# Steps of the mLSTM heads set behind the recurrence's bursts on TensorE

## The chip, the cores and the metric

One NeuronCore of a Trainium2 chip runs the whole program in one launch. The time is the device time of an execution in microseconds (us). TensorE (PE) multiplies, VectorE (DVE) and ScalarE (ACT) evict its results and do the elementwise work, GpSimd (POOL) does a little of it, SyncE (SP) issues the weight loads. [...]

## The reference

The input is 512 tokens of width 1024, in fp32. A first block has a hybrid token mixer, a cross attention to 256 memory rows and a gated FFN; a second block has three attention branches. The change touches the mixer alone. Half of the mixer's width is four mLSTM heads of 128 columns:

```
c_loc = einsum('bhclv,bhclk->bhcvk', v * wa[..., None], k)        # per chunk
c_new = s_old * c + s_loc * c_l                                   # state between chunks
p = exp(d - m_t) * einsum('bhctd,bhcsd->bhcts', q, k)
num = s_int * einsum('bhcvk,bhctk->bhctv', c_prev, q) + einsum('bhcts,bhcsv->bhctv', p, v)
h = num / max(|den|, exp(-m_t))                                   # then standardized per head
```

q, k, v and an output gate of each head are columns of `h @ w_in`. The other half is an RWKV-7 recurrence over eight heads of 64 (`state = state*w - (state kk)(kk a)^T + v k^T`), which is serial in time.

## The kernel before

The dense products split each fp32 operand in a high and a low part (`whi`, `wlo` of the weights, `hh`, `hl` of the activations) and take three products per 128 rows of weight: one *dense step* is three matmuls of 128x512 (`dense_steps`, `mmd`, L180). A block of 128 output columns is eight dense steps. ACT and DVE make `whi` and `wlo` from each loaded weight (L155, L158).

The mLSTM heads are two generators. `project(hd)` makes q, k, v and the gate of a head: four blocks, 32 dense steps; behind the k and q blocks `conv` does a width-4 convolution, on DVE three STTs (scalar_tensor_tensor instructions) of 128x512 (`k<-mc`, `q<-mc`) and one more (`k<-th`, `q<-th`). `attend(hd)` does the chunkwise attention of the head in ten steps, of which eight issue on TensorE: transposes of `cl` (the decay terms), transposes of `k2`, the product q k, four chunk steps c0 to c3, and, two empty steps later, the transposes of the normalized `Dm`. A chunk step c makes `vw` (weighted values, DVE, one buffer), the products `pn` (Vx by Dm), `pq` (C by q, from c1 on) and `pc` (vw by Kt, up to c2), then evicts: `nt` and the next state `C`, which `pq` of the next chunk step reads. Between c3 and the transposes of `Dm` some twenty small DVE instructions normalize the head.

`beside(gen, other, n)` joins the two: `project(hd + 1)` is the main stream, and `attend(hd)` is advanced by one step behind every third dense step (n = 32 // 10 = 3). Head 3's `attend` stands in the same way beside `mem_kv`, which makes keys and values for the cross attention and first needs the buffers `hh`.

`weave` interleaves that stream with the RWKV recurrence by progress. First comes `rwkv_inv`: a triangular solve in 31 rounds on DVE (`itmp`, `Tmat`, L158), with eight sets of four transposes of `Tmat` on TensorE. Then comes `rwkv_chain`: bursts of small matmuls that depend on each other through evictions: `columns` (transposes of BK and xT), `sides` (transposes of KR, products Z by Gm, copies to `rgu`), `solve` (rgu by TT, copies to `Z`), `step` (Z by St, q = 0 evicted by ACT, q = 1 by DVE: a copy to `Z` and one to `sg` or `yt`, L839), `ops` (St by Z, added to `St`). Between bursts `yield` lets the dense steps fill TensorE. In both stages `pinned` holds TensorE to the order in which the program is written; the queues of DVE and ACT are ordered by the scheduler, by priority in the order of writing and by readiness.

Of the kernel before, what the change touches and what calls it, by code (L numbers as in the profile page):

```python
# [41 lines left out]
MX = 2  # L42
# [21 lines left out]
            raise RuntimeError("every stream waits")  # L64


def beside(gen, other, n):

    for q, at in enumerate(gen):
        if q % n == n - 1:  # L70
            next(other, None)
        yield at
    for _ in other:
        pass


def weave(*gens):
    for _ in woven(*gens):
        pass


def part(gen, n):

    for _ in range(n):
        at = next(gen, "end")
        if at == "end":
            return
        yield at
# [11 lines left out]
class Build:  # L100
    def __init__(self, ctx, tc, ins, out):
        self.ctx, self.tc, self.nc = ctx, tc, tc.nc
        self.i, self.out = ins, out
        self.n = 0
        self.pinned = ""
        self.turns = ["p"]
        self.mms = ["mm"]
        self.const = ctx.enter_context(tc.tile_pool(name="const", bufs=1, reuse_waits=RW))

        self.wp = ctx.enter_context(tc.tile_pool(name="wp", bufs=2, reuse_waits=RW))  # L110
        self.wr = ctx.enter_context(tc.tile_pool(name="wr", bufs=2, side="right", reuse_waits=RW))
        self.banks = {}
        self.hb = ctx.enter_context(tc.tile_pool(name="hb", bufs=1))
        self.late = None
        self.before = None
# [26 lines left out]
    def units(self, n, gen, pri=0):  # L142

        q = 0
        while True:
# [4 lines left out]
            q += at is not None  # L150
            yield None if at is None else float(q) / n


    def act(self, out, in_, func=AF.Copy, **kw):
        self.pin("a", self.nc.scalar.activation(out, in_, func, **kw))  # L155
# [22 lines left out]
    def mmd(self, out, a, b, start, stop):  # L178

        ins = self.nc.tensor.matmul(out, lhsT=a, rhs=b, start=start, stop=stop)  # L180
        if "p" in self.pinned:
            self.pin("p", ins)
        elif self.before is not None:
            self.after(ins, self.before)
        self.before = ins.ins.name

    def mm(self, out, a, b, start=True, stop=True):
        self.pin("p", self.nc.tensor.matmul(out, lhsT=a, rhs=b, start=start, stop=stop))  # L188

    def tr(self, out, in_, ident=None):  # L190
        self.pin("p", self.nc.tensor.transpose(out, in_, self.ident if ident is None else ident))  # L191

    def after(self, ins, name):

        self.tc.add_manual_dep(ins.ins, name, mybir.DependencyInfo(
            mybir.DependencyClass.NoSync, mybir.DependencyReason.DATA), reason="dense order")
# [351 lines left out]
    def block(self, h, c0):  # L548
        wu = self.unit(self.i["w_in"][0][:, c0:c0 + 128], KD, 128)
        ps = self.pm()  # L550
        self.dense(ps, wu, h, range(KD))
        return ps
# [494 lines left out]
    def mlstm(self, ml, h, yT, hpool, kept):  # L1047
# [7 lines left out]
        def conv(ps, jb, tag):  # L1055
            cur = mt("mc", (128, 515), 1)
            nc.gpsimd.memset(cur[:, 0:3], 0.0)
            self.act(cur[:, 3:515], ps)
            acc = mt(tag, (128, 512), 2)
            self.act(acc, ps, AF.Identity, scale=v["m_conv_w"][:, 24 + jb:25 + jb], bias=v["m_conv_b"][:, jb:jb + 1])  # L1060
            for d in range(2, -1, -1):
                self.stt(acc, cur[:, d:d + 512], v["m_conv_w"][:, 8 * d + jb:8 * d + jb + 1], acc)
            th = mt("th", (128, 512), 1)
            self.act(th, acc, AF.Tanh, scale=0.5)
            self.stt(acc, th, 1.0, acc, OP.add, OP.mult)
            return acc
# [3 lines left out]
        def project(hd):  # L1070

            ps = yield from block(512 + 128 * hd)
            k2 = conv(ps, 4 + hd, "k2")
            ps = yield from block(128 * hd)
            q2 = conv(ps, hd, "q2")
            ps = yield from block(1024 + 128 * hd)
            vT = mt("vT", (128, 512), 1)
            self.act(vT, ps)
            og = yT[:, hd]
            gen = block(1536 + 128 * hd)  # L1080
            yield from part(gen, 3)
            p = self.pt("q")
            for c in range(NB):
                self.tr(p[:, 128 * c:128 * c + 128], vT[:, 128 * c:128 * c + 128])
            Vx = mt("Vx", (128, 4, 129), 2)
            nc.gpsimd.memset(Vx[:, :, 128:129], 1.0)
            self.act(Vx[:, :, 0:128], p.rearrange("p (c k) -> p c k", c=4))
            ps = yield from gen
            self.act(og, ps, AF.Tanh, scale=0.5)
            self.ts(og, og, 1.0, gh[:, hd:hd + 1], OP.add, OP.mult)  # L1090
            ops[hd] = (k2, q2, Vx)
# [80 lines left out]

        yield from project(0)
        for hd in range(3):
            yield from beside(project(hd + 1), attend(hd), 32 // (8 + MX))
        yield from beside(self.mem_kv(hpool, ml, kept), attend(3), 3)

    def sumsq(self, pool, x, g=None):

# [1037 lines left out]
```

## Time and profile before

| | us |
|---|---|
| time, median of 3 (lowest to highest) | 1542.51 (1539.69 to 1544.95) |
| the profiled execution, its own time | 1537.13 |
| its span, first to last instruction | 1535.4 |
| TensorE busy | 1506.9 |
| VectorE busy | 1082.0 |
| ScalarE busy | 748.7 |
| GpSimd busy | 98.9 |

The stage that the change touches lies at about 185 to 355 us of the span. A line of a timeline is the start, the duration, the engine, the source line, the operation, what it writes and reads, and its size; a bracket behind it is the idle time before it and what ended it. TensorE's matmuls overlap: the time that one takes of the engine is the distance to the next start, not its duration.

### The profile page before, as it was taken

To read this page: it belongs to the slowest core of one execution; us is meant where nothing else is said; L and a number is where in the kernel's file an instruction comes from. 1 tells how busy PE (TensorE), PEld (TensorE's weight loads), DVE (VectorE), ACT (ScalarE), POOL (GpSimd) and SP (SyncE) were. 2 spreads that over 40 slices of the span, in tenths; PEclk is the share of its full clock that TensorE was granted. 3 is DMA by queue.
4 is the path that set the end of the run, shared out by engine and by line. 5 is a ranking of instruction groups with operands and counts; after the bars stand their busy time and mean duration, and the time that the engine had idled before them with its cause. 6 is when DMAs were issued, how large, how long until landed. Compare 5 with 4: busy or idle time off the path is not lost.

```text
span 1535.4 us, 23728 instructions
## 1 busy us (share of the span) xinstructions
PE 1506.9 (98%) x8487; PEld 1237.2 (81%) x8487; DVE 1082.0 (70%) x2536; ACT 748.7 (49%) x1469; POOL 98.9 (6%) x241
## 2 busy tenths in 40 slices
PE   7999999999999999999999999999999999999999
PEld 5777788798888888888888888898877877878877
DVE  7776698998856556524544578879999785766563
ACT  6645556566554444434432444456554454644431
POOL 7000402122000000000000001000000000000000
PEclk9999999999999999999999999999999999999999
DMA  7533222145533133333333334242322322324222
GB/s 254 145 73 81 52 63 56 45 122 158 153 111 100 51 96 97 96 96 97 97 100 98 93 107 103 62 122 71 91 71 68 83 69 67 80 75 124 69 83 96
DMA packets 209591, 144.85 MB, mean 94 GB/s; under 512 B 13492, under 2 KB 190787, under 8 KB 208960
## 3 DMA queue, kind: packets, MB, share of 16 engines
q1 hardware_dynamic: 208000, 141.66, 32.6%
q0 software_dynamic: 1280, 1.52, 0.5%
q8 instruction: 67, 1.10, 0.3%
q14 instruction: 52, 0.43, 0.1%
q10 hardware_dynamic: 192, 0.14, 0.0%
HBM read 134.90 MB, written 8.39 MB: 93 GB/s over the span
## 4 chain that ended last, share of the span: by engine, by line
PE 85%; DVE 9%; ACT 2%; issue 1%; DMA 1%; DVEq 0%; SPq 0%; ACTq 0%
PE mm L180 39%; PE q L180 28%; PE p L188 4%; PE p L191 3%; PE y L188 3%; PE s L180 2%; DVE wlo L158 2%; PE s L188 2%; PE q L188 2%; PE s L191 1%; PE q L191 1%; DVE lqk L158 1%; DVE madd L1832 1%; ACT whi L155 1%; DVE m L1831 1%
## 5 line engine op out<-in xcount | busy, mean ns | idle before, releaser
L155 ACT ACTIVATE whi<-wraw 128x512 fp32r<-128x512 f32 (+2 forms) x472 | 292.5, 622 | 534.5 <-PE mm L180 216.2
L158 DVE TENSOR_TENSOR wlo<-wraw,whi 128x512 fp32r<-128x512 f32 (+2 forms) x472 | 320.3, 680 | 186.1 <-ACT whi L155 181.4
L180 PE MATMUL mm<-hh,whi 128*128 128x512 f32 (+1 forms) x760 | 281.2, 386 | 1.8 <-DVE hh L158 1.1
L180 PE MATMUL mm<-hh,wlo 128*128 128x512 f32 (+1 forms) x696 | 265.3, 381 | 0.0
L180 PE MATMUL mm<-hl,whi 128*128 128x512 f32 x632 | 247.2, 391 | 0.0
L180 PEld LDWEIGHTS mm<-hh,whi 128*128 128x128 f32 x760 | 138.9, 189 | 29.2 <-issue 3.0
L180 PEld LDWEIGHTS mm<-hh,wlo 128*128 128x128 f32 x696 | 131.0, 188 | 25.4
L180 PEld LDWEIGHTS mm<-hl,whi 128*128 128x128 f32 x632 | 119.2, 189 | 22.4 <-issue 0.5
L180 PE MATMUL q<-hh,whi 128*128 128x512 f32 x272 | 106.2, 391 | 0.0
L180 PE MATMUL q<-hh,wlo 128*128 128x512 f32 x272 | 106.0, 390 | 0.0
L180 PE MATMUL q<-hl,whi 128*128 128x512 f32 x272 | 106.0, 390 | 0.0
L180 PE MATMUL q<-whi,hh 128*128 128x512 f32 (+2 forms) x176 | 66.8, 388 | 0.0
L180 PE MATMUL mm<-whi,hh 128*128 128x512 f32 (+2 forms) x168 | 65.5, 396 | 0.0
L180 PE MATMUL q<-wlo,hh 128*128 128x512 f32 (+2 forms) x160 | 60.9, 381 | 0.0
L180 PEld LDWEIGHTS q<-hh,wlo 128*128 128x128 f32 x272 | 51.1, 188 | 10.6
L180 PEld LDWEIGHTS q<-hl,whi 128*128 128x128 f32 x272 | 51.1, 188 | 10.5
L180 PEld LDWEIGHTS q<-hh,whi 128*128 128x128 f32 x272 | 51.1, 188 | 10.4
L180 PE MATMUL mm<-wlo,hh 128*128 128x512 f32 (+2 forms) x152 | 57.9, 381 | 0.0
L180 PE MATMUL q<-whi,hl 128*128 128x512 f32 (+2 forms) x144 | 54.7, 380 | 0.0
L180 PE MATMUL mm<-whi,hl 128*128 128x512 f32 (+2 forms) x136 | 51.6, 380 | 0.0
L155 ACT ACTIVATE at_sm<-at_sm,at_mx 128x128 f32<-128x128 f32 (+3 forms) x64 | 35.7, 559 | 21.3 <-DVE at_mx L1598 20.9
L176 DVE SCALAR_TENSOR_TENSOR fy<-fc,vcols,fy 128x512 f32<-128x512 f32 x44 | 33.0, 751 | 9.2 <-ACT fy L155 8.5
(761 smaller groups left out, 3123.3 us busy)
## 6 DMA issues: line engine op xcount, KB each, us to landing
wraw<-in_w_in_dram SPq DMA_DIRECT2D x172, 256.0 KB, 2.9
wraw<-in_f_up_dram SPq DMA_DIRECT2D x88, 256.0 KB, 2.9
wraw<-in_f_down_dram SPq DMA_DIRECT2D x40, 256.0 KB, 2.8
wraw<-in_x_wkv_dram SPq DMA_DIRECT2D x32, 256.0 KB, 3.1
wraw<-in_w_out_dram SPq DMA_DIRECT2D x32, 256.0 KB, 2.7
wraw<-in_w_branch_dram SPq DMA_DIRECT2D x24, 256.0 KB, 2.7
wraw<-in_w_mem_kv_dram SPq DMA_DIRECT2D x16, 256.0 KB, 4.3
wraw<-in_x_wq_dram SPq DMA_DIRECT2D x16, 256.0 KB, 2.8
```

The source lines that it names most:

```text
L155: self.pin("a", self.nc.scalar.activation(out, in_, func, **kw))
L158: self.pin("v", self.nc.vector.tensor_tensor(out, a, b, op=op))
L176: self.pin("v", self.nc.vector.scalar_tensor_tensor(out, a, s, b, op0=op0, op1=op1))
L180: ins = self.nc.tensor.matmul(out, lhsT=a, rhs=b, start=start, stop=stop)
L188: self.pin("p", self.nc.tensor.matmul(out, lhsT=a, rhs=b, start=start, stop=stop))
L191: self.pin("p", self.nc.tensor.transpose(out, in_, self.ident if ident is None else ident))
L1831: nc.vector.max(m8, acc)
L1832: nc.vector.match_replace(acc, m8, acc, -3e38)
```

## The change

`beside` becomes a method. It still advances `attend` on average behind every third dense step, but each step may move: from two dense steps ahead of its place on, it is taken as soon as the last thing written on TensorE was not a dense product (the flag `burst`, set by `mm` and `tr`, cleared by `mmd`); two dense steps past its place it is taken in any case; two steps of `attend` have at least two dense steps between them.

```diff
-def beside(gen, other, n):
-    for q, at in enumerate(gen):
-        if q % n == n - 1:
-            next(other, None)
-        yield at
-    for _ in other:
-        pass
+    def beside(self, gen, other, n):
+        q = done = last = 0
+        while True:
+            if q - last > 1 and (q > n * (done + 1) + 1 or self.burst and q >= n * (done + 1) - 2):
+                next(other, None)
+                done += 1
+                last = q
+            at = next(gen, "end")
+            if at == "end":
+                break
+            q += 1
+            yield at
+        for _ in other:
+            pass
...
         self.before = ins.ins.name
+        self.burst = False
...
     def mm(self, out, a, b, start=True, stop=True):
         self.pin("p", self.nc.tensor.matmul(out, lhsT=a, rhs=b, start=start, stop=stop))
+        self.burst = True
...
-            yield from beside(project(hd + 1), attend(hd), 32 // (8 + MX))
-        yield from beside(self.mem_kv(hpool, ml, kept), attend(3), 3)
+            yield from self.beside(project(hd + 1), attend(hd), 32 // (8 + MX))
+        yield from self.beside(self.mem_kv(hpool, ml, kept), attend(3), 3)
```

`tr` sets the flag as `mm` does, and `__init__` clears it. Source lines move by 8 to 11. The same instructions are issued; the orders of SP and POOL do not change. Of the 32 steps of `attend` that issue on TensorE, 23 stood between two dense products and 9 ahead of a burst; now 22 stand behind a burst and 10 between dense products. The runs of dense products from the first to the last of them become 53 from 64.

The first place is TensorE at head 2's chunk step c2 (three products into one `q`) and the `step` burst beside it (`Z,St` into `y` and `p`). Before:

```order
L180 MATMUL mm_3238<-hh_83,wlo_3227 128x512
L188 MATMUL q_3247<-Vx_2819,Dm_2938 128x129
L188 MATMUL q_3247<-C_3183,q_2626 128x129
L188 MATMUL q_3247<-vw_3245,Kt_3012 128x129
L188 MATMUL y_3256<-Z_2782,St_2909 96x64 x4
L188 MATMUL p_3263<-Z_2782,St_2909 96x64 x4
L180 MATMUL mm_3238<-hh_83,whi_3228 128x512
```

And now:

```order
L188 MATMUL mm_3238<-hh_83,wlo_3227 128x512
L197 MATMUL y_3245<-Z_2782,St_2909 96x64 x4
L197 MATMUL p_3252<-Z_2782,St_2909 96x64 x4
L197 MATMUL q_3261<-Vx_2819,Dm_2992 128x129
L197 MATMUL q_3261<-C_3213,q_2615 128x129
L197 MATMUL q_3261<-vw_3259,Kt_3026 128x129
L188 MATMUL mm_3238<-hh_83,whi_3228 128x512
```

c2 stood ahead of the burst and now stands right behind it.

The second place is VectorE at the same point: the `vw` of c2 (`vw_3245` before, `vw_3259` now) and the two copies that evict the burst's second half (`Z` and `sg` from `p`). Before:

```order
L171 TENSOR_SCALAR vw_3245<-Vx_2819,ws 128x129
L158 TENSOR_TENSOR nt_3133<-qc_3180,q_3176 128x129
L176 SCALAR_TENSOR_TENSOR C_3183<-C_3140,dec,q_3176 128x129
...
L176 SCALAR_TENSOR_TENSOR q_3218<-mc_3215,vcols_576,q_3218 128x512
L176 SCALAR_TENSOR_TENSOR C_3254<-C_3183,dec,q_3247 128x129
L839 COPY Z_2783<-p_3263 64x4x64
L839 COPY sg<-p_3263 32x256
```

And now:

```order
L166 TENSOR_TENSOR nt_3159<-qc_3210,q_3206 128x129
L184 SCALAR_TENSOR_TENSOR C_3213<-C_3166,dec,q_3206 128x129
L184 SCALAR_TENSOR_TENSOR q_3218<-mc_3215,vcols_576,q_3218 128x512
L850 COPY Z_2783<-p_3252 64x4x64
L184 SCALAR_TENSOR_TENSOR q_3218<-mc_3215,vcols_576,q_3218 128x512
L850 COPY sg<-p_3252 32x256
L179 TENSOR_SCALAR vw_3259<-Vx_2819,ws 128x129
```

`vw` of c2 stood fourteen rows ahead of the copies and now stands behind both.

The third place is VectorE at head 0's chunk step c1: the state `C` that c1 leaves for c2 (`C_2185` before, `C_2228` now) and the convolution of the next head's q. Before:

```order
L158 TENSOR_TENSOR nt_2154<-qc_2182,q_2178 128x129
L176 SCALAR_TENSOR_TENSOR C_2185<-C_2161,dec,q_2178 128x129
...
L176 SCALAR_TENSOR_TENSOR q_2195<-mc_2192,vcols_576,q_2195 128x512
L158 TENSOR_TENSOR Tmat<-Tmat,itmp 128x22x10
L176 SCALAR_TENSOR_TENSOR q_2195<-mc_2192,vcols_576,q_2195 128x512
```

And now:

```order
L184 SCALAR_TENSOR_TENSOR q_2184<-mc_2181,vcols_576,q_2184 128x512
L179 TENSOR_SCALAR vw_2243<-Vx_1867,ws 128x129
L184 SCALAR_TENSOR_TENSOR q_2184<-mc_2181,vcols_576,q_2184 128x512
L166 TENSOR_TENSOR nt_2164<-qc_2225,q_2221 128x129
L184 SCALAR_TENSOR_TENSOR q_2184<-mc_2181,vcols_576,q_2184 128x512
L184 SCALAR_TENSOR_TENSOR C_2228<-C_2171,dec,q_2221 128x129
```

`C` stood ahead of the three convolution STTs and now stands behind them; head 1 has the same.

## Rows read from the trace of the kernel before

**Rows 1.** The page's first line, and its chain that ended last by engine.
```profile
span 1535.4 us, 23728 instructions
...
PE 85%; DVE 9%; ACT 2%; issue 1%; DMA 1%; DVEq 0%; SPq 0%; ACTq 0%
```

**Rows 2.** A window: us, busy PE, PEld, DVE, ACT, POOL, clock, DMA, GB/s.
```profile
280.00:300.00 20.00, 20.00 (x231) 16.55 (x230) 18.98 (x70) 11.01 (x23) 3.34 (x7) 1.00 0.15 42
```

**Rows 3.** All waits of TensorE, 180 to 360 us: total, times, longest.
```profile
PE mm L180 <- DVE hh L158: 1.1, 1, 1.1
PE mm L180 <- ACT hh L155: 0.7, 1, 0.7
PE y L188 <- DVE Z L807: 0.3, 1, 0.3
PE q L191 <- DVE Dm L173: 0.2, 1, 0.2
```

**Rows 4.** Timeline of TensorE, head 2's steps c1 and c2.
```profile
278.04 0.38 PE L188 MATMUL q<-Vx,Dm 128*128 128x129 f32 x2
...
278.62 0.48 PE L180 MATMUL mm<-hh,whi 128*128 128x512 f32 x1
278.94 0.40 PE L180 MATMUL mm<-hl,whi 128*128 128x512 f32 x1
279.17 0.40 PE L180 MATMUL mm<-hh,wlo 128*128 128x512 f32 x1
...
282.02 0.38 PE L188 MATMUL q<-Vx,Dm 128*128 128x129 f32 x2
...
282.68 0.81 PE L188 MATMUL y<-Z,St 128*96 128x64 f32 x8
283.33 0.84 PE L188 MATMUL p<-Z,St 128*96 128x64 f32 x8
```

**Rows 5.** Timeline of VectorE, the same steps.
```profile
279.22 0.26 DVE L171 TENSOR_SCALAR vw<-Vx,ws 128x129 f32<-128x129 f32 x1
...
282.99 0.75 DVE L176 SCALAR_TENSOR_TENSOR q<-mc,vcols,q 128x512 f32<-128x512 f32 x1
...
284.90 0.41 DVE L839 COPY Z<-p 64x256 f32<-64x256 f32 x1
285.34 0.42 DVE L839 COPY sg<-p 32x256 f32<-32x256 f32 x1
```

**Rows 6.** Timeline of VectorE, head 1's state C and the q convolution.
```profile
239.55 1.54 DVE L176 SCALAR_TENSOR_TENSOR q<-mc,vcols,q 128x512 f32<-128x512 f32 x2 [0.44 <-ACT q L155]
...
241.87 0.35 DVE L176 SCALAR_TENSOR_TENSOR C<-C,dec,q 128x129 f32<-128x129 f32 x1
```

**Rows 7.** Timeline of TensorE, further places.
```profile
238.34 0.60 PE L191 MATMUL p<-ident,Tmat 128*32 128x128 f32 x4
...
250.63 0.60 PE L191 MATMUL q<-ident,Dm 128*128 128x128 f32 x4
251.07 0.60 PE L191 MATMUL y<-ident,KR 128*128 128x128 f32 x4
251.60 0.65 PE L188 MATMUL p<-Z,Gm 32*32 32x64 f32 x32
...
258.32 1.17 PE L188 MATMUL p<-St,Z 32*64 32x96 f32 x15
...
310.95 0.62 PE L188 MATMUL y<-St,Z 32*64 32x96 f32 x9 [0.33 <-DVE Z L807]
...
349.44 1.09 PE L191 MATMUL q<-ident,Dm 128*128 128x128 f32 x4
```

**Rows 8.** Timeline of VectorE, what those places wait for.
```profile
250.56 0.69 DVE L767 COPY Z<-p 32x512 f32<-32x512 f32 x1
...
258.12 0.69 DVE L807 COPY Z<-s 32x512 f32<-32x512 f32 x1
...
310.92 0.69 DVE L158 TENSOR_TENSOR wlo<-wraw,whi 128x512 fp32r<-128x512 f32 x1
```

More of the change, by code (lines that the diff above doesn't have):

```diff
@@ L185, in mmd @@
         self.before = ins.ins.name
+        self.burst = False
     def mm(self, out, a, b, start=True, stop=True):
         self.pin("p", self.nc.tensor.matmul(out, lhsT=a, rhs=b, start=start, stop=stop))
+        self.burst = True
     def tr(self, out, in_, ident=None):
         self.pin("p", self.nc.tensor.transpose(out, in_, self.ident if ident is None else ident))
+        self.burst = True
     def after(self, ins, name):
```

## The prediction

> **What bounds the kernel now.** I read the page's first line and its chain of waits first: the reader sees one core with a span of 1535.4 us, and a chain that runs over TensorE for 85% and over VectorE for 9% [rows 1]. Then busy time by windows, in the stage that the change touches: in 280 to 300 us TensorE is busy for all of its 20.00 us at full clock (1.00), VectorE for 18.98 and ScalarE for 11.01 [rows 2]. So TensorE is the bound, and VectorE is close behind it: what becomes late on VectorE has little room. Third, the waits of TensorE between 180 and 360 us: only 2.3 us in all, of which 1.1 and 0.7 are for the buffers `hh`, 0.3 for a `Z` copy of the recurrence, 0.2 for the transposes of `Dm` [rows 3]. The change moves neither the need for `hh` nor the work of any engine. It can save at most the other 0.5 us of waits, slow starts that the view does not call waits, and what a change from dense products to small ones costs in itself. Last I read timelines of TensorE and VectorE at each place where the new order differs, and went through them by hand: when is the operand ready, and when does TensorE now come to it?
>
> **Part 1: fewer breaks in the dense products (64 runs become 53).** Rows 4 hold one break alone and one ahead of a burst. Head 2's c1, alone between dense products, starts at 278.04 and the next dense matmul at 278.62: 0.58. That matmul lasts from 278.62 to 278.94, 0.32, where the next takes 0.23 (to 279.17), so 0.09 more; together 0.67. c2, which runs straight into a burst, takes 282.02 to 282.68 = 0.66 [rows 4]. The break thus costs 0.01 net; its bounds are nothing and the whole 0.09 of the slow start. Eleven breaks fewer: bounds 0 and −1.0 us, and I take −0.1 (the row of c2 is the very case wanted: small products attached to a burst).
>
> **Part 2: head 2's `vw` behind the burst's copies.** c2 has stood ahead of the burst and now comes right behind it; its `vw`, made at 279.22, long before use [rows 5], now stands behind both copies of the burst's second half on VectorE, as the order shows. I count from the start of the `p` products (283.33). They take to +0.84 [rows 4]; then come the `Z` copy, 0.44 (284.90 to 285.34), a q convolution STT of 0.75, the `sg` copy of 0.42 and `vw` of 0.26 [rows 5]: 2.7. TensorE leaves the burst at about +0.65 (as 283.33 − 282.68) and does `pn` and `pq`, 0.22 each (two thirds of 0.66): it wants `vw` at 1.09. Wait: **+1.6 us**. Bounds: 0 (if VectorE has the STT behind it by then and ScalarE's half lets the copies start earlier) and 1.7. What hides it if not this? Nothing: the dense product behind c2 is queued behind the waiting `pc` on the same engine.
>
> The rows show VectorE in the order `vw`, STT, copies, as the program has it [rows 5]. [...] No row here shows VectorE out of order.
>
> **Part 3: the state `C` of c1, heads 0 and 1.** `C` now stands behind three q convolution STTs. Head 1's c1 now comes behind the transposes of `Tmat`, which started at 238.34; with its own 0.66 taken out ahead of them they start at 237.68 and, at the 0.44 that four transposes take to the next start (250.63 to 251.07) [rows 7], c1 takes 238.12 to 238.78. Three dense steps later (9 × 0.23 + 0.09 = 2.16, rows 4) comes c2: `pn` at 240.94, `pq`, which reads `C`, at 241.16. On VectorE the STTs waited 0.44 for ScalarE's eviction of the q block (239.55), and the `C` behind the third of them started at 241.87 and took 0.35 [rows 6]. The same row of work now starts 0.66 earlier, since that block ends so much earlier, with a `vw` of 0.2 in it (0.26 less the overlap): 241.87 − 0.66 + 0.2 = 241.41, done at 241.76. Wait: 0.6. Head 0 has the same order with a little more room: 0.5. Together **+1.1**. Bounds: 0 (the STTs start earlier) and 2 × 1.6 (as in part 2, when all of VectorE's queue is late).
>
> **Part 4: head 1's `Dm`.** c3 comes two dense steps later (6 × 0.23 = 1.4), so the normalization that follows it on VectorE is later, and the `Z` copy behind that (250.56, 0.69, done at 251.25) as well [rows 8]. The product of `Z` and `Gm` reads it at 251.60, with 0.35 to spare [rows 7]; and it now stands ahead of the transposes of `Dm` (250.63), not behind, so TensorE comes to it 0.44 earlier. The wait is between 0.1 (0.44 − 0.35: VectorE is not late) and 1.5 (the 1.4 arrives in full). I take **+0.6**, a little under the middle, since VectorE had some idle time here, as the 0.44 ahead of the STTs [rows 6].
>
> **Part 5: `cl`'s transposes.** St by `Z` at 258.32 [rows 7] starts before its `Z` copy (258.12, 0.69, so 258.81) is done [rows 8]; its later matmuls thus wait for it. The transposes of head 2's `cl`, 0.44 as in part 3, stood ahead of it and filled that time; now they come behind: **+0.44** (bounds 0 and 0.5).
>
> **Part 6: behind the `hh` wait.** St by `Z` at 310.95 waits 0.33 for its copy [rows 7]. On VectorE a `wlo` of 0.69, which starts at 310.92 behind that copy [rows 8], now stands ahead of the second copy. The copy is up to 0.69 later; I put at 0.2 what passes while TensorE still does the products of the other copy: **+0.5**, by the nearer end. Bounds 0 and 0.7.
>
> **Part 7: what is saved.** The transposes of `Dm` now start behind a burst, later. Head 2's wait of 0.2 [rows 3] goes, and with it the slow run behind it, which I take to be like head 3's: −0.5. Head 3's (349.44) take 1.09 where those at 250.63 take 0.60 [rows 7]: −0.49, but the product of St and `Z` behind it then waits itself for some 0.3: −0.2. Bounds: nothing, and −1.0 for both.
>
> SP and POOL keep their orders, no instruction is added, and no DMA is issued in another place; those cost nothing, since the dense products they feed keep their sequence.
>
> **The sum.** 1.6 + 1.1 + 0.6 + 0.44 + 0.5 − 0.5 − 0.2 − 0.1 = 3.4 us. The profiled execution took 1537.1 us (span 1535.4), so the profiled time would be 1540.5. The median of the runs is 1542.5, 5.4 above that execution; 1542.5 + 3.4 = **1545.9 us**, 0.22% slower. What a measurement of this kernel can tell from no change is about 0.3%, 4.6 us, so the forecast is no change that can be told, on the slow side. The forecast's own range, with the bounds of parts 2 to 6 (half of what they span, as they will not all fall to one side), is 1543 to 1548.
>
> **Rivals.**
>
> *Slower: steps wait at full price wherever they follow a burst.* One mechanism: VectorE evicts the burst first, as the recurrence's copies have the older priority, and the step of `attend` behind it finds its operand a full eviction late. Place: c2 in heads 0 and 1 and `Z` by `Gm` of part 4, beside head 2's. Price: 1.6 instead of 0.6 and 0.5 at two places and 1.1 (three quarters of the 1.4) instead of 0.6 at the third, 2.6 more: +6.0, so 1548.5. It decides from 4.6 us, that is when two of these three places pay in full. For it: VectorE is busy for 18.98 of 20 us [rows 2]. Against it: ScalarE, which gates the convolution, has room there (11.01 of 20). Chance 0.28.
>
> *The waits don't appear.* VectorE's small lag is made up since the convolution STTs run as soon as ScalarE is through, and the waits of parts 2 to 6 shrink to nothing. What is left are the gains: −0.5 for head 2's `Dm`, −0.5 for head 3's, −1.0 for breaks at their bound: −2, so 1540.5. For it: in 175 us of this stage TensorE waits for VectorE hardly at all [rows 3], so operands are mostly early. Against it: the order puts `vw` and `C` behind work of over 1.5 us. Chance 0.14.
>
> *The change does more: a break costs more than the starts show.* If the small products, alone, also held back dense products behind them, 11 breaks at 0.3 (the first dense start of rows 4 counted in full) would give −3.3, and with the gains of part 7 some −4.5 to −5: 1538. For it: the slow first dense start. Against it: 0.67 and 0.66 for the same step alone and attached [rows 4]. Chance 0.06.
>
> **How the numbers follow.** The forecast has 0.52, the slow rival 0.28, the waits that don't appear 0.14, the dear breaks 0.06. Slower by over 0.3% (above 1547.1): 0.21 of the slow rival and 0.10 of the forecast, whose upper end passes 1547.1: 0.31. Faster: 0.05 of the dear breaks and 0.03 of the rival before it: 0.08. Within 0.3%: the rest, 0.61. The range is 1540 to 1551: below, it ends at the rival without waits, above, 2.5 us past the slow rival, which is what the median of before stands below its highest run (1544.95).
>
> **What would show it.** In the waits of TensorE from 180 to 360 us the total rises from 2.3 to about 6 us, with new rows: `q` for `vw` (some 1.6, head 2), `q` for `C` (two, some 0.5 to 0.6 each), `p` for `Z` longer or new; the row `q` for `Dm` is gone. Dense matmuls keep 0.23 from start to start. Wrong would be: no wait for `vw` (part 2 falls, with it half of the sum); waits for `C` over 1 us each (the slow rival); a touched stage shorter than before by over 2 us without any wait gone (the dear breaks).

## The result, and the profile after

The changed kernel takes 1551.68 us (median of 4 runs, 1550.78 to 1553.58); before, in the runs on the same chip, 1541.1 us (1539.11 to 1544.95). The ratio is 1.0072, with a 95% interval of 1.0055 to 1.0088: 10.6 us slower. The forecast was 1545.9, at most 1551. The direction is as forecast, the size is three times the 3.4 us of the sum.

The page's first line and its chain of waits after answer to [rows 1]:

```profile
span 1550.5 us, 23729 instructions
...
PE 83%; DVE 10%; ACT 3%; issue 2%; DMA 1%; DVEq 0%; SPq 0%; ACTq 0%
```

The waits of TensorE, 188 to 370 us (engine, line, releaser: total, times, longest), answer to [rows 3]:

```profile
PE mm L188 <- DVE hh L166: 1.8, 1, 1.8
PE q L197 <- DVE vw L179: 1.5, 1, 1.5
PE q L197 <- DVE C L184: 0.9, 2, 0.5
PE p L197 <- DVE Z L778: 0.8, 1, 0.8
PE y L197 <- ACT Z L163: 0.8, 1, 0.8
PE y L197 <- DVE Z L818: 0.4, 2, 0.2
PE p L197 <- DVE Z L818: 0.4, 1, 0.4
```

The sum is 6.6 us, where it was 2.3; the prediction had "about 6". (The window leaves out 0.9 us of waits for head 0's `cl` at 183 us: run e2 below, with head 0 as before, has them too, 0.5 and 0.4.) So the waits are much as worked out, and yet what they grew by, 4.3 us, is not half of the 10.6 us. The windows of TensorE behind the wait for `hh` show the rest (us, busy PE, PEld, DVE, ACT, POOL, granted clock, DMA share, GB/s):

```profile
316.00:318.00 2.00, 0.47 (x3) 0.47 (x4) 2.00 (x5) 1.34 (x3) 0.00 (x0) 1.00 0.14 43
318.00:320.00 2.00, 2.00 (x21) 2.00 (x19) 1.97 (x5) 0.75 (x2) 0.00 (x0) 0.78 0.84 240
320.00:322.00 2.00, 2.00 (x9) 1.53 (x8) 0.93 (x4) 0.59 (x1) 0.40 (x1) 0.50 1.02 296
...
326.00:328.00 2.00, 2.00 (x11) 2.00 (x11) 1.94 (x4) 0.60 (x1) 0.88 (x1) 0.50 0.00 0
328.00:330.00 2.00, 2.00 (x13) 2.00 (x13) 0.24 (x1) 0.48 (x1) 1.88 (x4) 0.66 0.00 0
330.00:332.00 2.00, 2.00 (x20) 2.00 (x19) 0.80 (x1) 1.58 (x4) 0.39 (x2) 1.00 0.03 8
```

TensorE is idle for most of 316 to 318, and from about 319.1 to 329.4 us its granted clock is 0.50 (0.55 in 319.1 to 319.2, 0.50 in 319.2 to 329.3, 0.75 in 329.3 to 329.4; 0.78 and 0.66 in the windows at the two ends). Three dense products of 128x256 take 0.64 us there (327.53 to 328.17) and 0.36 behind it (329.41 to 329.77). In the first profile of before the same place ran at 1.00, also in a window with as busy a DMA:

```profile
308.00:310.00 2.00, 2.00 (x23) 1.91 (x21) 1.94 (x6) 1.25 (x3) 0.40 (x1) 1.00 0.96 282
```

Note the busy column: it reads 2.00 at a clock of 0.50 (326 to 328) as at 1.00 (330 to 332), so a table of busy time alone does not show this.

To see where the time is lost, I matched the same numbered dense product (the products into `mm`, 2088 in each trace) in the two timelines and took how much later it starts than in the first profile of before. The table has what each stage adds to that, in us; stages are in the times of before. "Before, again" is a second profile of the unchanged kernel (run e6 below), and shows what chance does.

| stage of before, us | changed | before, again |
|---|---|---|
| 0 to 59 (start) | +5.4 | +3.8 |
| 59 to 185 | 0.0 | +1.5 |
| 185 to 220 (head 0) | +1.1 | +1.3 |
| 220 to 247 (head 1) | +1.0 | 0.0 |
| 247 to 262 (`Dm` of head 1, `cl` of head 2) | +1.5 | 0.0 |
| 262 to 290 (`vw` of head 2) | +1.8 | 0.0 |
| 290 to 307 (up to and with the `hh` wait) | +0.2 | +0.1 |
| 307 to 320 (behind the `hh` wait) | +4.4 | +1.1 |
| 320 to 1464 | +1.3 | +0.9 |

The first profile of before was an execution with a quick start: its 1537.13 us lie 4 below the median. The start, and part of the stage at 185 to 220, are chance. What the change adds in this profile is 220 to 320: 8.8 us, with at most 1 more from head 0. Of the 4.4 behind the `hh` wait some may be chance: the unchanged kernel's second profile adds 1.1 there, with some 3 us at half clock.

The predicted places, one by one. First c2 of head 2, on TensorE ([rows 4] of before):

```profile
291.42 0.84 PE L197 MATMUL p<-Z,St 128*96 128x64 f32 x8
292.10 0.44 PE L197 MATMUL q<-Vx,Dm 128*128 128x129 f32 x2
292.37 0.39 PE L197 MATMUL q<-C,q 128*128 128x129 f32 x2
294.30 0.49 PE L197 MATMUL q<-vw,Kt 128*128 128x129 f32 x2 [1.54 <-DVE vw L179]
```

And VectorE there ([rows 5]):

```profile
292.42 0.41 DVE L850 COPY Z<-p 64x256 f32<-64x256 f32 x1
292.75 0.73 DVE L184 SCALAR_TENSOR_TENSOR q<-mc,vcols,q 128x512 f32<-128x512 f32 x1
293.51 0.42 DVE L850 COPY sg<-p 32x256 f32<-32x256 f32 x1
293.95 0.29 DVE L179 TENSOR_SCALAR vw<-Vx,ws 128x129 f32<-128x129 f32 x1
```

`vw` is done at 294.24, 2.8 us behind the start of the `p` products at 291.42; the prediction had 2.7. VectorE runs the four rows in the order that the program has: `vw` starts at 293.95, 0.44 behind the start of the `sg` copy and not ahead of it. Next head 1's state `C` ([rows 6]): VectorE makes it from 247.89 on, for 0.34, behind the third convolution STT.

```profile
247.22 0.75 DVE L184 SCALAR_TENSOR_TENSOR q<-mc,vcols,q 128x512 f32<-128x512 f32 x1
247.89 0.34 DVE L184 SCALAR_TENSOR_TENSOR C<-C,dec,q 128x129 f32<-128x129 f32 x1
```

TensorE at that place, at the `Dm` of head 1, at the `cl` of head 2, and behind `hh` ([rows 7]); the bracket is the wait and its releaser:

```profile
248.29 0.49 PE L197 MATMUL q<-C,q 128*128 128x129 f32 x2 [0.47 <-DVE C L184]
...
259.60 0.64 PE L197 MATMUL p<-Z,Gm 32*32 32x64 f32 x30 [0.80 <-DVE Z L778]
...
267.30 0.62 PE L197 MATMUL p<-St,Z 32*64 32x96 f32 x9 [0.36 <-DVE Z L818]
...
315.37 0.38 PE L188 MATMUL mm<-hh,whi 128*128 128x256 f32 x1
317.53 0.39 PE L188 MATMUL mm<-hh,whi 128*128 128x256 f32 x1 [1.78 <-DVE hh L166]
...
322.80 0.58 PE L197 MATMUL y<-St,Z 32*64 32x96 f32 x4 [0.75 <-ACT Z L163]
323.55 1.05 PE L197 MATMUL y<-St,Z 32*64 32x96 f32 x9 [0.17 <-DVE Z L818]
```

Every wait that was forecast is there. What the prediction did not look at is VectorE ahead of the split of `hh`. Before:

```profile
301.31 0.68 DVE L158 TENSOR_TENSOR sg<-sg,gag 128x512 f32<-128x512 f32 x1
302.03 0.42 DVE L791 COPY rgu<-p 32x256 f32<-32x256 f32 x1
...
303.84 0.41 DVE L839 COPY Z<-y 64x256 f32<-64x256 f32 x1
...
305.98 2.49 DVE L158 TENSOR_TENSOR hh<-wraw,hh 128x512 fp32r<-128x512 f32 x4
```

After:

```profile
312.51 0.42 DVE L802 COPY rgu<-p 32x256 f32<-32x256 f32 x1
...
313.12 0.89 DVE L166 TENSOR_TENSOR sg<-sg,gag 128x512 f32<-128x512 f32 x1
...
314.73 0.41 DVE L850 COPY Z<-y 64x256 f32<-64x256 f32 x1
...
316.80 2.49 DVE L166 TENSOR_TENSOR hh<-wraw,hh 128x512 fp32r<-128x512 f32 x4
```

The normalization step `sg`, 0.68 to 0.89 us, stood ahead of the last copy that the `solve` burst waits for, and now stands behind it. The split of `hh` now comes 4.29 us behind that copy instead of 3.95. On TensorE, the place before:

```profile
303.52 1.08 PE L188 MATMUL p<-rgu,TT 32*32 32x128 f32 x32
305.26 0.38 PE L180 MATMUL mm<-hh,whi 128*128 128x256 f32 x1 [0.67 <-ACT hh L155]
306.73 0.39 PE L180 MATMUL mm<-hh,whi 128*128 128x256 f32 x1 [1.08 <-DVE hh L158]
```

And after, ahead of the rows shown above:

```profile
313.62 1.08 PE L197 MATMUL p<-rgu,TT 32*32 32x128 f32 x32
314.63 0.65 PE L201 MATMUL q<-ident,cl 128*128 128x128 f32 x4
```

The transposes of head 3's `cl`, which stood behind this place, now fill the first wait, for 0.74 us, and the wait for VectorE is longer by as much. So the idle time in front of the dense products is one piece of 1.78 us, where it was 0.67 and 1.08: hardly more in sum (1.75), but not broken by a product.

### The profile page after: what moved, and what is told of

Its sections match the earlier page's. It is cut to its first block, busy times and chain, and to the rows that moved or that the text cites. A ratio compares the mean times of both kernels' runs of the same rounds, so it can differ in the third digit from the quotient of the medians.

```text
span 1550.5 us, 23729 instructions
## 1 busy us (share of the span) xinstructions
PE 1513.9 (98%) x8487; PEld 1242.0 (80%) x8487; DVE 1084.6 (70%) x2536; ACT 748.2 (48%) x1469; POOL 95.7 (6%) x241
## 4 chain that ended last, share of the span: by engine, by line
PE 83%; DVE 10%; ACT 3%; issue 2%; DMA 1%; DVEq 0%; SPq 0%; ACTq 0%
PE mm L188 39%; PE q L188 27%; PE p L197 4%; PE p L201 3%; PE y L197 3%; DVE wlo L166 2%; PE s L188 2%; PE s L197 2%; PE q L197 2%; PE s L201 1%; PE q L201 1%; ACT whi L163 1%; DVE lqk L166 1%; DVE madd L1843 1%; DVE rs_t L166 1%
## 5 line engine op out<-in xcount | busy, mean ns | idle before, releaser
L188 PEld LDWEIGHTS q<-hh,wlo 128*128 128x128 f32 x272 | 51.1, 188 | 10.6
```

## The experiments

Theory A: the 10.6 us are the predicted waits, and about half of it TensorE's low clock behind the wait for `hh`. Theory B: the clock there is incidental, the price is spread over all moved steps. Theory C: the longer start of the profile is part of the change. All times below are medians beside runs of before on the same chip.

**e1: head 3 as before.**

```diff
-        yield from self.beside(self.mem_kv(hpool, ml, kept), attend(3), 3)
+        yield from self.beside_old(self.mem_kv(hpool, ml, kept), attend(3), 3)
```

> The changed order for heads 0 to 2, the order of before for head 3 beside the keys and values. Theory A (about half of the 10.6 us is TensorE at half clock in the 10 us behind the wait for hh, 4 to 5 us with the Z waits there, the rest are the waits of heads 0 to 2): the clock stays at 1.00 behind the hh wait, and the time is 5 to 6 us above before (1546 to 1547), with the waits for vw (1.5) and C (0.9) still there. Theory B (the price is spread over all moved steps alike, the clock only happens to be low in that profile): 8 to 9 us above before, since only a quarter of the steps go back. Theory C (the 5.4 us by which the first 53 us of the profile were longer is part of the change): 10 us above before.

1546.71 against 1541.09 us, ratio 1.0042 (1.0027 to 1.0057): +5.6, the time that A gave, but not for A's reason. The profile has the low clock behind `hh` all the same:

```profile
300.00:345.00 45.00, 42.54 (x449) 38.92 (x448) 37.54 (x101) 24.57 (x52) 6.63 (x16) 0.89 0.30 89
```

and its wait for `hh` is 0.7 + 1.8, as `sg` stands behind the copy here too. The moved steps of head 3 are thus not needed for it. In the profiled execution (1547.6) the stage at 307 to 320 adds 3.9 us; the six executions spread from a mean clock of 0.990 to 0.994, so in some of them there may have been less of it. Theory C falls: the start is 1.2 us over that of the first profile here, 3.8 in e6.

**e2: only head 3 moved** (`beside_old` for heads 0 to 2 instead).

> The reverse: heads 0 to 2 as before, only head 3's steps moved. Theory A: 4 to 5 us above before, granted clock at half for some 10 us behind the wait for hh, no wait for vw and none for C of heads 0 and 1. Theory B: 2 to 3 us above before. Theory C: 10 us above before, as the first 53 us would be long here too.

1543.2 against 1541.09, ratio 1.0012 (1.0001 to 1.0024): +2.1, which B had named. The waits for `Z` are there (1.1 and 0.6), the wait for `hh` is 1.1, the clock over 300 to 345 is 0.96, as in the second profile of before. So head 3 costs its waits, and the long stretch at half clock needs the other heads' order. The two halves give 7.7 us of the 10.6.

**e3: two buffers for `vw`.**

```diff
-                    vw = mt("vw", (128, 129), 1)
+                    vw = mt("vw", (128, 129), 2)
```

> The changed kernel with two buffers for vw instead of one, so that head 2's vw of c2 need not stand behind the burst's copies. TensorE's order is the changed one. Theory A: the wait of 1.5 us for vw is gone, the rest stays: 1.5 us below the changed kernel, 9 above before, with the half clock behind hh still there. If VectorE as a whole is what is late (theory B), the wait moves on to the next operand, and the time stays within 0.5 us of the changed kernel's.

1550.01 against 1541.09, ratio 1.0051 (1.0033 to 1.0068): +8.9, as A gave. The wait for `vw` is gone from the view and did not move on: the stage 262 to 290 adds −0.05 instead of 1.8. The waits for `C` (1.0) and `hh` (1.7) and the low clock (0.85) stay.

**e4: 16 transposes ahead of the `hh` wait.**

```diff
                 ps = self.pm()[:, 0:256]
+                if m == 0:
+                    for _ in range(16):
+                        self.tr(ps[:, 0:128], self.ident)
```

> The changed kernel with 16 more transposes of the identity (128x128, 1.8 us at 0.44 for four) on TensorE directly ahead of the first dense product that waits for hh; their result is overwritten by that product. ScalarE's order changes by one place with it: a Z copy comes ahead of the next whi. Theory A (the clock falls because TensorE stands idle for 1.8 us there): TensorE is busy through the wait, the clock stays at 1.00 for the 10 us behind, and the time is 4 to 5 us below the changed kernel, 6 above before, though TensorE has more work. Theory B (the clock has no part in the 10.6 us): as the changed kernel or up to 1 us slower, the transposes being added to the wait's end.

1546.19 against 1541.09, ratio 1.0037 (1.0023 to 1.0051): 5.5 us less than the changed kernel, for more work on TensorE. The transposes take 1.67 us, the wait left is 0.39:

```profile
312.96 1.91 PE L201 MATMUL mm<-ident 128*128 128x128 f32 x16
314.63 0.36 PE L188 MATMUL mm<-hh,whi 128*128 128x256 f32 x1
315.39 0.38 PE L188 MATMUL mm<-hh,whi 128*128 128x256 f32 x1 [0.39 <-DVE hh L166]
```

and the clock behind it:

```profile
300.00:345.00 45.00, 43.99 (x517) 40.10 (x513) 41.52 (x118) 27.11 (x57) 10.44 (x18) 1.00 0.32 95
```

The stage up to and with the `hh` wait adds 0.3 (0.2 in the changed kernel), the one behind it 0.0 instead of 4.4. The waits for `Z` in it are still 0.8 us in sum, so between these two profiles it is the clock that gave the 4.4 us back. Theory B, by which the transposes could gain nothing, falls. But a profile is one execution. Over all of them the mean clock is 0.9933 here and 0.9918 in the changed kernel: at the 1 us for 0.001 of the last section that is 1.6 of the 5.5 us. By another estimate it is 2.2: 0.0016 of the span is 4.9 us more at 0.50, if the clock is 1.00 otherwise, and three products that take 0.64 us at 0.50 and 0.36 at 1.00 lose 0.44 of such time. What the rest of the 5.5 us is, beside the spread of the medians, is not shown.

**e5: the same transposes in the kernel before.**

> The kernel before with the same 16 identity transposes ahead of the wait for hh. In before, TensorE's wait there is 0.67 + 1.08 us in the one profile, and the executions spread from 1538.2 us at a granted clock of 0.997 to 1545.3 at 0.991. Theory A (idle time at this place lowers the clock, in before in a part of the executions): the executions above 1542 become fewer, median 1 to 2 us below before. Theory A' (the clock of before falls elsewhere, at the start): same median within 1 us. If the transposes cost TensorE more than the wait that they fill: up to 1 us above.

1540.4 against 1541.17, ratio 0.9998 (0.9989 to 1.0007): no difference. The clock in 300 to 345 is 1.00, and no execution of 12 has a mean clock under 0.993 (25 of the 93 of before do), but the median is where theory A' had it and not 1 to 2 us lower as A said: there was little to win, and this is not a faster version.

**e6: the kernel before again.**

> The kernel before once more, unchanged, for a second profile and as a measure of the spread: ratio 1.000 within 0.0015. The profile tells whether the first 53 us, and the stretch behind the hh wait, differ from one execution of the same program to the next: if the 5.4 us longer start of the changed kernel's profile is chance, this profile's start differs from the first one's by some us as well.

1543.08 against 1541.17, ratio 1.0009 (0.9998 to 1.002), the spread of this measurement. Its profiled windows at the start, at 185 to 215 and behind `hh` show that all three vary by chance; the first profile of before had 0.97, 0.94 and 1.00:

```profile
0.00:60.00 60.00, 45.82 (x208) 36.33 (x209) 43.51 (x106) 35.97 (x71) 27.99 (x63) 0.91 0.67 216
185.00:215.00 30.00, 30.00 (x203) 24.92 (x203) 19.92 (x49) 12.81 (x26) 8.34 (x5) 0.84 0.18 45
300.00:345.00 45.00, 43.04 (x474) 39.23 (x473) 40.67 (x118) 26.55 (x56) 10.87 (x19) 0.96 0.34 100
```

**e7: both mends, e3 and e4.**

> The changed kernel with both mends, two buffers for vw and the 16 transposes ahead of the hh wait. If the two prices add (theory A): 8.9 + 5.1 - 10.6 = 3.4 us above before, 1544.5. What is left then are the waits for C (0.9), for Z (0.8 and some 1) and the clock's dip at 190 us. If the wait for vw only moves to a later place, 5 us above before, as with the transposes alone.

1543.37 against 1541.17, ratio 1.0015 (1.0003 to 1.0026): +2.2, below the 3.4 of a plain sum. Beside e3 the transposes are worth 6.7 us here; beside e4 the second buffer is worth 2.9 (both by the difference to before). What is left answers to the waits for `C` (1.0), and for `Z`. The filling does not always hold the clock: in this profile it is 0.96 over 300 to 340 (some 3 us at half clock, by 0.04 of 40 us, twice), with 0.3 us left of the wait for `hh` and `y` waiting up to 0.6 for `Z`, and the stage behind `hh` adds 1.5.

**e8: head 2 as before, heads 0, 1 and 3 moved.**

> The changed order for heads 0, 1 and 3, the order of before for head 2. Head 2's normalization on VectorE is the last thing ahead of the split of hh there. Theory A with VectorE's backlog from head 2 as the reason for the longer wait at hh: the vw wait (1.5) is gone, the wait for hh is back to 1.1 us behind ScalarE's part, the clock behind it mostly at 1.00: 4 to 5 us above before. If the backlog comes from heads 0 and 1, or from head 3's own cl ahead of hh: 8 to 9 us above before, and the clock at half there.

1544.91 against 1541.17, ratio 1.0021 (1.0011 to 1.003): +3.7 by the medians, +3.2 by the ratio; theory A had 4 to 5. `vw` does not wait, the wait for `hh` is 1.1, and VectorE has `sg` ahead of the copy again. The clock:

```profile
300.00:345.00 45.00, 42.22 (x476) 37.96 (x475) 40.88 (x117) 27.12 (x56) 11.32 (x19) 1.00 0.34 100
```

The mean clock of its ten executions is 0.994, as that of before beside it. So the places of head 2's steps put the split of `hh` late, and with them the low clock goes.

**e9: the chunk steps c0 to c3 stay, the others move; e10: only the chunk steps move.** In `beside`, the steps of `hold` go to the place of before (`q >= n * (done + 1)`, ahead of the `yield`); e9 shown, in e10 it is `(0, 1, 2, 7, 8, 9)`:

```diff
+        hold = (3, 4, 5, 6)
...
-            if q - last > 1 and (q > n * (done + 1) + 1 or self.burst and q >= n * (done + 1) - 2):
+            if done not in hold and q - last > 1 and (q > n * (done + 1) + 1 or self.burst and q >= n * (done + 1) - 2):
```

> The changed placement for the transposes of cl, of k2 and of Dm and for the product q k; the chunk steps c0 to c3 of all heads stay at the places of before. Theory A (what is late are operands that VectorE makes for the chunk steps and, through the later c3, its backlog at hh): no wait for vw or C, granted clock 1.00 behind the hh wait, time within 2 us of before. If any step behind a burst is the trouble: 4 to 6 us above before.

> The complement: only c0 to c3 move behind bursts, the transposes and q k stay. Theory A: the waits for vw (1.5) and C (0.9) as in the changed kernel, the wait for hh 1.5 to 1.8 us on VectorE and the clock at half behind it; 6 to 9 us above before. If the transposes carry most of the price: 1 to 3 us above before.

e9: 1549.47 against 1542.54, ratio 1.004 (1.0027 to 1.0052), 6.9 us slower, a clear miss for "within 2 us". The profile is of the fastest of its 11 executions (1545.21, mean clock 0.994; eight of the others are at 0.991 or lower), so it does not show where the median's time goes. There is no wait for `vw` or `C`, but new ones, at c0 of head 1 and at the transposes of `Dm` of head 2:

```profile
238.81 0.46 PE L200 MATMUL q<-Vx,Dm 128*128 128x129 f32 x2 [1.00 <-ACT th L166]
...
306.24 1.10 PE L204 MATMUL q<-ident,Dm 128*128 128x128 f32 x4 [1.80 <-DVE Dm L184]
```

q k had moved to the later side and c0 not, so between the two there was one dense step where before had three. They are joined by an STT on VectorE, `Dm`, which the program has behind three of the k convolution; the bracket names `th`. e10: 1556.49, ratio 1.0085 (1.0069 to 1.0101), 13.95 us slower, worse than the whole change, with 3.49 us at the `Dm` of head 3 that no theory had:

```profile
369.03 1.24 PE L204 MATMUL q<-ident,Dm 128*128 128x128 f32 x4 [3.49 <-DVE Dm L184]
```

That profile is of its slowest execution, and TensorE is slow behind that wait too, up to about 378 us: three products of 128x256 take 0.64 us at 373.76, and 0.36 ahead of the wait at 362.20. The stage 320 to 360 of before adds 6.9 us, twice the wait. So it is not the chunk steps as such. Each step reads what VectorE or ScalarE made of the one before, and with either subset moved, some pair came closer together.

**e11: steps may move to the early side only.**

```diff
-            if q - last > 1 and (q > n * (done + 1) + 1 or self.burst and q >= n * (done + 1) - 2):
+            if q - last > 1 and (q > n * (done + 1) - 1 or self.burst and q >= n * (done + 1) - 2):
```

> The changed placement with the window on the early side alone: a step of attend goes behind a burst up to two dense steps ahead of its old place, and at its old place in any case. No chunk step comes later than before, so c3 and the normalization are not late at hh. Theory A: no half clock behind hh, waits for C or vw at most 0.5 us; between 1 us below and 2 us above before. If standing behind a burst is what costs, whichever side it came from: 4 us or more above before.

1548.69 against 1542.54, ratio 1.0035 (1.0023 to 1.0047), 6.2 us slower. No chunk step ahead of the `hh` wait is late, and yet the wait for `hh` is 1.8 and the clock in 300 to 345 is 0.89; in VectorE's order `sg` stands behind the copy. My reason for the late split, a later c3, falls with this run. What e1, e3, e11 and the changed kernel share, and before, e2 and e8 have not, is the place of `sg`. It is not the only way: e10 has `sg` at its old place, a wait of 0.7 + 1.5, and a clock of 0.89 too.

**e12: the kernel before, with the first split of `hh` made twice.**

```diff
             self.split_from(md[:, 0, ks].rearrange("p k t -> p (k t)"), md[:, 1, ks].rearrange("p k t -> p (k t)"), raw)
+            if q == 0:
+                self.sub(md[:, 1, ks].rearrange("p k t -> p (k t)"), raw, md[:, 0, ks].rearrange("p k t -> p (k t)").bitcast(F32))
```

> The kernel before, with the order of TensorE untouched, and VectorE's first split of hh (0.62 us) made twice, so that the wait of TensorE for hh is 0.6 us longer: 0.7 for ScalarE and 1.7 for VectorE, as in the run with head 3 as before. One whi and wlo change places with a Z copy behind it. Theory A (the idle time there, beyond what before has, takes TensorE to half clock for 5 to 10 us): granted clock well under 1.00 in the 40 us behind the wait in the profile, time 3 to 5 us above before, for 0.6 us of VectorE's work. Rival (the clock follows something else that the changed order does to TensorE): 0.6 to 1 us above before, clock 1.00 or 0.96 as in before.

1545.62 against 1541.47, ratio 1.0023 (1.0012 to 1.0035): +4.2 by the medians for 0.62 us of VectorE's work, as A gave. But the profile, of an execution of 1543.67, has a longer wait than was meant (0.7 + 2.3, not 1.7) and no low clock, against A:

```profile
300.00:345.00 45.00, 41.84 (x483) 38.32 (x481) 41.55 (x121) 27.93 (x59) 10.95 (x19) 1.00 0.34 101
```

Seven of the 12 executions lie at 1545.2 to 1547.1 with a mean clock of 0.990 or 0.991, the other five at 1540.2 to 1544.0 with 0.993 to 0.996; of the 17 of before beside them one is as low as 0.991. That fits a low clock behind the wait in some executions and not in others. No trace of one of the seven was taken, so this is not shown, and what brings the clock down stays open: of idle time there, 1.75 us in sum was followed by no half clock or by some 3 us of it in before, 1.78 by 10 us in the changed kernel, 3.0 by none in this profile.

## Why the prediction was wrong

- **Part 1, fewer breaks (−0.1):** not contradicted. In e3, where `vw` does not wait, the stage 262 to 290 with its moved steps is 0.05 us shorter than before; fewer breaks gave nothing that shows, and the rival of dear breaks falls.
- **Part 2, `vw` (+1.6):** 1.54 us, and 1.8 for the stage; e3 took it away and the time fell by 1.7. Right.
- **Part 3, `C` (0.6 and 0.5):** 0.47 each. Right.
- **Parts 4 and 5, `Z` behind `Dm`, and `cl` (0.6 and 0.44):** 0.80 and 0.36. Right; the stage adds 1.5.
- **Part 7, the gain at `Dm` (−0.5 and −0.2):** the dense products gain 0.5 between 290 and 303 us (10.57 us late, then 10.11). For head 3 nothing shows (0.1).
- **Part 6, behind the `hh` wait (+0.5, bounds 0 and 0.7): this is the step that failed.** The waits for `Z` there are 0.17 behind VectorE's `wlo`, as it said, and 0.75 for ScalarE's copy, which now stands behind a `whi` and which it had not looked at: together more than its upper bound. But the stage lost 4.4 us, because TensorE fell to half clock for some 10 us. The prediction read the clock as 1.00 in [rows 2] and carried it through the sum as if the change could not touch it; it had no term and no rival for it, though [rows 3] showed 1.8 us of idle time at one place. It also took that place as untouched ("the change moves neither the need for `hh`..."), where the two waits became one. The profiles show the size, 4.4 us in the changed kernel and 0.0 with the idle time filled (e4); the medians fell by 5.5 there and by 6.7 in e7 beside e3, more than the clock can account for. e8 shows that head 2's new place brings it. Why the clock fell here, with no more idle time in sum than before, stays open.

The sum as it came out, by the runs: 5.5 for the `hh` place (e4), 2.9 for `vw` with the filling in (e4 to e7), 2.2 left for all other waits and gains (e7): 10.6 us. These are differences of medians one behind the other, so they must add up, and each is uncertain by 2 us or more. The profile of the changed kernel has 4.4 behind the `hh` wait, 1.8 for `vw` and 2.7 for the rest of 220 to 307 us. The predicted terms other than those at `hh` and `vw` were 1.1 + 0.6 + 0.44 − 0.8 = 1.3.

By the count of waits the slow rival was wrong too: `C` did not wait 1.6 us anywhere. Its 1548.5 was nearer by the size alone.

## What to carry to other kernels

Steps that depend on each other through another engine's work want an even distance on TensorE: in each of the nine variants that moved steps TensorE had a wait for VectorE or ScalarE that was not there before, and each was slower, by 2.1 (e2) to 13.95 us (e10). When moving instructions, look at the one place that already has idle time, not only at the places that are moved: here its sum stayed the same (1.75 and 1.78 us), and yet the clock behind it fell to 0.50, and that stage lost 4.4 us, more than any single wait (1.78). Sixteen worthless transposes in the gap were cheaper than the gap (e4, 5.5 us less by the medians; in the kernel before, e5, no difference). And take two profiles of the kernel before: one execution was several us off the median (1537.13 against 1541.1) at places that the change never touches.

## What the runs showed of the hardware

One idle stretch of 1.8 us on TensorE was followed, 1.6 us later (317.53 to 319.1), by about 10 us at half clock (0.50 in 319.2 to 329.3), and the stage lost more than twice that idle time (4.4 us). Of the 14 profiles, five have a single idle piece of 1.5 to 1.8 us at this place (the changed kernel, e1, e3, e10, e11), and all five have 10 to 14 us at half clock behind it (a mean of 0.85 to 0.89 over 300 to 345); e12, with 2.3 us, has none; the eight others, with 1.1 us or less, have none or 3 to 4 us (1.00 or 0.96). The same program shows it or not from one execution to the next: before has none in one profile and some 3 us in the other, and over 93 executions of before the mean granted clock goes from 0.991 to 0.997, and the mean time with it from 1545.2 to 1539.0 us. That is about 1 us for each 0.001; of the 9.25 us between the lowest and the highest of the 93 (1537.43 and 1546.68) 6.2 go with the clock.
